# The MLP's second matrix as products of 400 and 264 columns, with the lesser operands of 128 tokens as weights

## The chip, the cores and the metric

The kernel runs on one core of one Trainium2 chip. The metric is the device time of one execution in microseconds (us), the median of several runs. A core has a tensor engine (PE, with its weight loads shown as PEld), a vector engine (DVE), a scalar engine (ACT), GpSimd (POOL) and SyncE (SP), which here only issues DMAs. Each engine works through its own instructions in order and waits for others by semaphores.

## The reference, cut to what matters

One step of a decoder with four layers, 264 tokens (256 of a prompt, 8 samples) and 1024 channels, all in float32. Each layer is a mixer (layers 0 and 3: gated short conv, 1: pooling, 2: Conformer conv), then an MLP:

```
x = x + mixer(rms_norm(x))
h = relu(rms_norm(x) @ mlp_w1)        # 1024 -> 4096
x = x + (h * h) @ mlp_w2              # 4096 -> 1024
```

At the end stands one more norm. The change concerns `(h * h) @ mlp_w2` in all four layers.

## The kernel before, in words

Channels lie on the 128 partitions and the 264 tokens along the free axis, so x is eight blocks of 128 x 264. TensorE takes float32 in its one-pass form only with a loss, so each number is split into a leading part (h, rounded) and a lesser part (l = number - h), and a product is three matmuls into one sum: whi with uh, whi with ul, wlo with uh (lines 160, 161, 162, the helper `mm`). The product of the two lesser parts is left out.

Weights come as a stream of units of 1024 rows x 256 columns (1 MB), in the order of their use: SP's DMA into `wst` (3 buffers), ACT's cast to `whi` (line 119), DVE's difference to `wlo` (line 120; POOL's in one mixer), into 5 buffers. Each unit is split in four pieces; `behind` issues some pieces (`pump`) behind each block of matmuls, and `done_units` allows the next unit's pieces. All of the order is written out by hand: what `behind` issues is in program order on each engine's queue.

The MLP goes in two halves of the hidden layer (h = 0, 1). In a half the first matrix makes 16 hidden blocks u (DVE line 1076, ACT 1082, split by ACT 225 and DVE 227). Then comes the stage of the second matrix (lines 1107 to 1120): for each of 4 pairs of output blocks (j), over 16 hidden blocks in two units (g), the 3 matmuls of 264 columns each for both blocks. When an output block is complete, `summed` adds it to x on DVE (line 1104 in the first half, `add_x`, line 532, in the second). In the second half `ready` follows: ACT scales x to xh (230) and squares it (242), DVE makes xl (232), POOL adds the squares in `acc` (243). The next mixer starts with `opening_unit`, which uses xh and xl block by block, and then a matmul on `acc` (272). There are 8 such stages. Behind the last stage `last_ready` (1218) squares and scales x, and `to_rows` (1204), queued in `later`, turns it with three transposes on PE (1212).

Layer 2's mixer runs a conv of 31 taps. DVE sums the taps of some blocks (855); PE takes those of the others by diagonal matrices (928 to 930), which ACT (814) and POOL (808) make one tap at a time (`make_diag`). They lie in places of other tiles (`diag_place`), and a new one is issued as a step uses one up.

## Time and profile before

| what | value |
|---|---|
| device time, median of 3 runs | 1126.05 us (1123.84 to 1126.81) |
| span of the profiled execution, first to last instruction | 1120.6 us |
| PE busy | 1101.6 us, 98%, 8981 matmuls |
| DVE, ACT, POOL busy | 762.3, 635.9, 197.7 us |
| chain that ended last | PE 91%, DVE 5%, ACT 2%, POOL 1% |
| DMA queue of the weights | 185.86 MB, 52.3% of 16 engines |

The span leaves out what lies before the first and behind the last instruction; the median of the runs is 5.45 us longer. The profiled execution has no time of its own beside its span. A matmul's busy time in a row (about 284 ns) is its way through the array; matmuls overlap, so the time that one takes from the next is read from the distance between starts, or from the length of a stretch over the number of matmuls in it.

### The profile page before, as it was taken

The page shows a single profiled execution, that of the slowest core. Times are in us where ns is not written, and L with a number is a line of the kernel's source. Part 1 is how long each engine was busy: PE and PEld are TensorE (multiplying, and loading weights), DVE is VectorE, ACT ScalarE, POOL GpSimd, SP SyncE. Part 2 cuts the span into 40 slices and gives each one's busy share as a digit, 9 for nine tenths or more (in the row PEclk, how much of TensorE's full clock was granted, in tenths as well). Part 3 has the DMA queues.
Part 4 walks back from the last instruction along what each step waited for, and adds up shares of the span by engine and source line. Part 5 has one row for each costly group of instructions (what it writes and reads, how often), then busy time and mean ns, then how long its engine had stood idle before and what let it go on. Part 6 is the DMA issues. An engine that isn't in the chain of part 4 may idle for free.

```text
span 1120.6 us, 22403 instructions
## 1 busy us (share of the span) xinstructions
PE 1101.6 (98%) x8981; PEld 1094.9 (98%) x8981; DVE 762.3 (68%) x1471; ACT 635.9 (57%) x1380; POOL 197.7 (18%) x363
## 2 busy tenths in 40 slices
PE   9999999999999999999999999999999999999997
PEld 8999999999999999999999999999999999999997
DVE  6878865566569647666998697467568687656731
ACT  5556663565458536644895686356545466535642
POOL 4212420100220000014895100000011120000010
PEclk9999999999999999999999999999999999999998
DMA  7666765555508666554440076655536555565511
GB/s 252 226 218 185 242 205 165 181 181 174 166 5 262 215 193 208 166 182 146 151 120 1 3 244 214 191 178 189 188 114 226 188 174 176 181 191 185 184 44 39
DMA packets 182792, 189.13 MB, mean 169 GB/s; under 512 B 3439, under 2 KB 181015, under 8 KB 182664
## 3 DMA queue, kind: packets, MB, share of 16 engines
q1 hardware_dynamic: 182288, 185.86, 52.3%
q0 software_dynamic: 384, 1.81, 0.5%
q8 instruction: 70, 1.15, 0.4%
q14 instruction: 34, 0.28, 0.1%
q10 hardware_dynamic: 16, 0.03, 0.0%
HBM read 186.27 MB, written 2.89 MB: 169 GB/s over the span
## 4 chain that ended last, share of the span: by engine, by line
PE 91%; DVE 5%; ACT 2%; POOL 1%; issue 0%; DMA 0%; SPq 0%; DVEq 0%; ACTq 0%
PE mm L160 28%; PE mm L162 28%; PE mm L161 28%; DVE mm L855 2%; PE mm L343 1%; ACT diag L814 1%; PE mm L341 1%; PE mm L344 1%; POOL wlo L120 1%; DVE gb L879 0%; PE mm L928 0%; POOL diag L808 0%; PE mm L929 0%; PE mm L930 0%; DMA vrows<-in_norm_mix_g_dram 0%
## 5 line engine op out<-in xcount | busy, mean ns | idle before, releaser
L119 ACT CAST whi<-wst 128x512 fp32r<-128x512 f32 x692 | 386.9, 616 | 250.1 <-PE mm L161 236.3
L120 DVE TENSOR_TENSOR wlo<-wst,whi 128x512 fp32r<-128x512 f32 x652 | 430.7, 705 | 99.6 <-ACT whi L119 91.7
L160 PE MATMUL mm<-xh,whi 128*128 128x264 f32 x1512 | 434.8, 288 | 3.1 <-DVE t L870 3.1
L162 PE MATMUL mm<-xh,wlo 128*128 128x264 f32 x1512 | 430.6, 285 | 0.0
L161 PE MATMUL mm<-xl,whi 128*128 128x264 f32 x1512 | 429.1, 284 | 0.0
L160 PE MATMUL mm<-uh,whi 128*128 128x264 f32 x1168 | 332.5, 285 | 0.0
L162 PE MATMUL mm<-uh,wlo 128*128 128x264 f32 x1168 | 331.6, 284 | 0.0
L161 PE MATMUL mm<-ul,whi 128*128 128x264 f32 x1168 | 331.1, 283 | 0.0
L160 PEld LDWEIGHTS mm<-xh,whi 128*128 128x128 f32 x1512 | 285.6, 189 | 4.1 <-DVE t L870 3.8
L161 PEld LDWEIGHTS mm<-xl,whi 128*128 128x128 f32 x1512 | 286.2, 189 | 0.2
L162 PEld LDWEIGHTS mm<-xh,wlo 128*128 128x128 f32 x1512 | 285.3, 189 | 0.0
L160 PEld LDWEIGHTS mm<-uh,whi 128*128 128x128 f32 x1168 | 220.0, 188 | 0.2 <-DVE xall L534 0.2
L161 PEld LDWEIGHTS mm<-ul,whi 128*128 128x128 f32 x1168 | 219.8, 188 | 0.0
L162 PEld LDWEIGHTS mm<-uh,wlo 128*128 128x128 f32 x1168 | 219.5, 188 | 0.0
L243 POOL TENSOR_TENSOR acc<-acc,sq 128x264 f32<-128x264 f32 x62 | 53.3, 860 | 552.2 <-ACT sq L242 551.4
L1076 DVE SCALAR_TENSOR_TENSOR t<-mm,r 128x264 f32<-128x264 f32 x128 | 55.1, 430 | 65.9 <-PE mm L162 65.8
L225 ACT CAST uh<-u 128x264 fp32r<-128x264 f32 x144 | 59.6, 414 | 32.1 <-DVE u L589 28.0
L1082 ACT ACTIVATE u<-t 128x264 f32<-128x264 f32 x128 | 54.1, 423 | 35.6 <-DVE t L1076 35.6
L855 DVE SCALAR_TENSOR_TENSOR mm<-gb,pv,mm 128x256 f32<-128x256 f32 x144 | 58.6, 478 | 7.1 <-POOL gb L878 2.5
L227 DVE TENSOR_TENSOR ul<-u,uh 128x264 fp32r<-128x264 f32 x144 | 61.6, 428 | 0.3
L532 DVE TENSOR_TENSOR xall<-mm,xall 128x264 f32<-128x264 f32 x48 | 20.6, 430 | 59.8 <-PE mm L162 59.8
L120 POOL TENSOR_TENSOR wlo<-wst,whi 128x512 fp32r<-128x512 f32 x40 | 53.2, 1356 | 21.0 <-ACT whi L119 21.0
(210 smaller groups left out, 826.0 us busy)
## 6 DMA issues: line engine op xcount, KB each, us to landing
wst<-in_mlp_w_dram SPq DMA_DIRECT2D x128, 1024.0 KB, 5.6
wst<-in_a_w_in_dram SPq DMA_DIRECT2D x23, 1024.0 KB, 5.4
wst<-in_c_w_pw_dram SPq DMA_DIRECT2D x12, 1024.0 KB, 5.5
wst<-in_a_w_out_dram SPq DMA_DIRECT2D x8, 1024.0 KB, 5.1
xin<-in_x_prompt_dram SPq DMA_DIRECT2D x2, 512.0 KB, 6.8
wst<-in_b_w_group_dram SPq DMA_DIRECT2D x1, 1024.0 KB
out_y_prompt_dram<-ys SPq DMA_DIRECT2D x4, 256.0 KB
stc<-in_state_conv_c_dram SPq DMA_DIRECT2D x2, 480.0 KB, 6.7
```

Source lines behind the costliest of these rows:

```text
L119: nc.scalar.copy(hi[:, k:k + 2], st[:, k:k + 2])
L120: (nc.gpsimd if u == 3 or (u, k) in ((0, 2), (0, 6)) else lo_engine[0]).tensor_tensor(out=lo[:, k:k + 2], in0=st[:, k:k + 2], in1=hi[:, k: ...
L160: nc.tensor.matmul(ps[:, :n], hi[:, k, s], xh[:, :n], start=first, stop=False)
L161: nc.tensor.matmul(ps[:, :n], hi[:, k, s], xl[:, :n], start=False, stop=False)
L162: nc.tensor.matmul(ps[:, :n], lo[:, k, s], xh[:, :n], start=False, stop=last)
L225: nc.scalar.copy(h, src)
L227: lambda: nc.vector.tensor_tensor(out=l, in0=src, in1=h.bitcast(F32), op=ALU.subtract)
L243: nc.gpsimd.tensor_tensor(out=acc, in0=acc, in1=sq, op=ALU.add)
L532: nc.vector.tensor_tensor(out=x[k], in0=ps[:, :T], in1=x[k], op=ALU.add)
L855: nc.vector.scalar_tensor_tensor(out=z(e), in0=gb[e][:, t:t + SEQ], scalar=col("ccw", t * 8 + e), in1=z(e), op0=ALU.mult, op1=ALU.add,)
L1076: nc.vector.scalar_tensor_tensor(out=t1, in0=ps[:, :T], scalar=0.0, in1=r, op0=ALU.max, op1=ALU.mult)
L1082: nc.scalar.activation(u, t1, AF.Square)
```

## The change

The hidden block's leading and lesser parts now lie side by side in one tile of 528 columns. Units of the second matrix have 512 rows and 512 columns. A stage has two quarters (q) of four output blocks each. Per hidden block and output block there are two matmuls: whi with 400 columns (264 leading ones and the lesser ones of the first 136 tokens), wlo with 264. The lesser parts of the last 128 tokens are the *weights* of one further matmul per hidden block, with the 512 columns of whi moving; its sums, tokens by outputs, lie in a bank `turned`. ACT copies these to `back` (two casts of 128 x 256), and one matmul with an identity for each output block (`turn`) adds them, turned back, to the block's last 128 columns. `summed` then adds two parts to x.

```diff
+OWN = T - 128
     def hidden(n):
-        return (
-            [act.tile([P, T], F32R, tag=f"uh{m}", name=f"uh{m}") for m in range(n)],
-            [act.tile([P, T], F32R, tag=f"ul{m}", name=f"ul{m}") for m in range(n)],
-        )
+        both = [act.tile([P, 2 * T], F32R, tag=f"u{m}", name=f"u{m}") for m in range(n)]
+        return [t[:, :T] for t in both], [t[:, T:] for t in both], both
...
             def summed(e, ps):
+                nc.vector.tensor_tensor(out=x[e][:, :OWN], in0=ps[:, T:T + OWN], in1=x[e][:, :OWN], op=ALU.add)
                 if h == 1:
                     return add_x(e, ps, ready)
...
-            for j in range(4):
-                ps2 = [psum(), psum()]
-                for g in range(2):
-                    w = next_unit()
-                    for c in range(2):
-                        for k in range(NB):
-                            kk = g * NB + k
-                            mm(ps2[c], w, c, k, uh[kk], ul[kk], T, kk == 0, kk == 15)
-                        if c == 1:
-                            done_units()
-                        if g == 0:
-                            behind(lambda c, ps: lambda: None, c, None)
-                        else:
-                            behind(summed, 2 * j + c, ps2[c], h == 1 and j == 3 and c == 1)
+            for q in range(2):
+                last_parts(h, q, both, summed)
+
+    def last_parts(h, q, both, summed):
+        turned, pss, back = psum(), [], []
+        def turn(c):
+            nc.tensor.matmul(
+                pss[c][:, OWN:T], back[c // 2][:, c % 2 * P:(c % 2 + 1) * P], ident_r, start=False, stop=True
+            )
+        for g in range(4):
+            hi, lo = (wide(t) for t in next_unit())
+            for k in range(4):
+                nc.tensor.matmul(
+                    turned, both[4 * g + k][:, T + OWN:], hi[:, k], start=g + k == 0, stop=g + k == 6
+                )
+            if g == 3:
+                for n in range(2):
+                    back.append(tmp.tile([P, 2 * P], F32R, tag="u", name="back"))
+                    nc.scalar.copy(back[n], turned[:, n * 2 * P:(n + 1) * 2 * P])
+            for c in range(4):
+                if g == 0:
+                    pss.append(psum())
+                s = slice(c * P, (c + 1) * P)
+                for k in range(4):
+                    t = both[4 * g + k]
+                    nc.tensor.matmul(pss[c][:, :T + OWN], hi[:, k, s], t[:, :T + OWN], start=g + k == 0, stop=False)
+                    nc.tensor.matmul(pss[c][:, :T], lo[:, k, s], t[:, :T], start=False, stop=False)
+                if c == 3:
+                    done_units()
+                ready_now = ()
+                if g == 3 and c > 0:
+                    for n in ((0, 1), (2,), (3,))[c - 1]:
+                        turn(n)
+                    ready_now = ((0, 1), (2,), (3,))[c - 1]
+                if not ready_now:
+                    behind(lambda c, ps: lambda: None, c, None, False, 1)
+                for n in ready_now:
+                    behind(summed, 4 * q + n, pss[n], h == 1 and q == 1 and n == 3, 1)
```

An ACT copy at the start makes the identity in the one-pass type (`ident_r`). Because the hidden tiles are now joined, the places of other tiles in them move too: the pooling mixer's rows, and in layer 2 the conv's diagonals, of which fewer are made before the conv, with a longer lead in it:

```diff
-                    for _ in range(4 if e < 4 else 3):
+                    for _ in range(3 if e < 7 else 2):
                         make_diag()
...
-            if made[0] - 16 <= taps.index((e, t)):
+            if made[0] - 20 <= taps.index((e, t)):
                 make_diag()
```

The order of PE in the last stage; before, in the first unit of the last pair, between the products for output block 6 and those for block 7 (`xall` is x, `ident` the identity, line 1212 the transposes of block 5):

```order
L160 MATMUL mm<-uh_13125,whi 128x264
L161 MATMUL mm<-ul_13141,whi 128x264
L162 MATMUL mm<-uh_13125,wlo 128x264
L1212 MATMUL mm<-ident,xall 128x128 x3
L160 MATMUL mm<-uh_13118,whi 128x264
L161 MATMUL mm<-ul_13134,whi 128x264
```

And now, in the last unit behind the second of its four output blocks (lines 1161 and 1162 are the two products, 1141 is `turn`, 1265 the transposes of x):

```order
L1161 MATMUL mm<-u_12472,whi 128x400
L1162 MATMUL mm<-u_12472,wlo 128x264
L1141 MATMUL mm<-ident_r,back 128x128 x2
L1265 MATMUL mm<-ident,xall 128x128 x3
L1161 MATMUL mm<-u_12469,whi 128x400
L1162 MATMUL mm<-u_12469,wlo 128x264
```

Before, block 5 was complete 24 matmuls ahead of its transposes; now the transposes are of block 4, whose last sums come from the first of the two matmuls of line 1141 right ahead of them.

The order of DVE at the end of layer 0's MLP, from output block 5's add on; before (532 is the add to x, 120 the weights' lesser parts, 232 makes xl):

```order
L532 TENSOR_TENSOR xall<-mm,xall 128x264
L120 TENSOR_TENSOR wlo<-wst,whi 128x512 x2
L232 SCALAR_TENSOR_TENSOR xl_133<-xall,pv,xh_125 128x264
L120 TENSOR_TENSOR wlo<-wst,whi 128x512 x2
L232 SCALAR_TENSOR_TENSOR xl_134<-xall,pv,xh_126 128x264
L120 TENSOR_TENSOR wlo<-wst,whi 128x512 x2
L532 TENSOR_TENSOR xall<-mm,xall 128x264
L120 TENSOR_TENSOR wlo<-wst,whi 128x512 x2
L532 TENSOR_TENSOR xall<-mm,xall 128x264
L232 SCALAR_TENSOR_TENSOR xl_135<-xall,pv,xh_127 128x264
L232 SCALAR_TENSOR_TENSOR xl_136<-xall,pv,xh_128 128x264
```

And now (1125 and 547 are the two adds to x, 128 the weights' lesser parts, 247 makes xl):

```order
L1125 TENSOR_TENSOR xall<-mm,xall 128x136
L547 TENSOR_TENSOR xall<-mm,xall 128x264
L128 TENSOR_TENSOR wlo<-wst,whi 128x512
L247 SCALAR_TENSOR_TENSOR xl_133<-xall,pv,xh_125 128x264
L1125 TENSOR_TENSOR xall<-mm,xall 128x136
L547 TENSOR_TENSOR xall<-mm,xall 128x264
L247 SCALAR_TENSOR_TENSOR xl_134<-xall,pv,xh_126 128x264
L1125 TENSOR_TENSOR xall<-mm,xall 128x136
L547 TENSOR_TENSOR xall<-mm,xall 128x264
L247 SCALAR_TENSOR_TENSOR xl_135<-xall,pv,xh_127 128x264
L247 SCALAR_TENSOR_TENSOR xl_136<-xall,pv,xh_128 128x264
```

The adds of blocks 4 to 7 moved together, each is two instructions, and the pieces of weights that lay between them moved ahead.

## Rows read from the trace of the kernel before

**Rows 1.** The page's busy times, and from its 40 slices PE's busy tenths and the clock granted to TensorE.

```profile
PE 1101.6 (98%) x8981; PEld 1094.9 (98%) x8981; DVE 762.3 (68%) x1471; ACT 635.9 (57%) x1380; POOL 197.7 (18%) x363
...
PE   9999999999999999999999999999999999999997
...
PEclk9999999999999999999999999999999999999998
```

**Rows 2.** Waits of PE alone, longest in total first (engine, line, tile, what it waited for: us in total, times, longest).

```profile
PE mm L160 <- DVE t L870: 3.1, 3, 1.9
...
PE mm L928 <- POOL diag L808: 1.0, 1, 1.0
...
PE st L949 <- POOL diag L808: 0.8, 1, 0.8
```

**Rows 3.** Windows of three of the eight stages of the second matrix (stretch, its length, busy us and instructions of PE, PEld, DVE, ACT, POOL, then clock, DMA share, GB/s); a stage has 384 matmuls, three more straddle its ends.

```profile
159.29:205.91 46.62, 46.62 (x387) 46.62 (x386) 24.20 (x42) 18.20 (x34) 0.00 (x0) 1.00 0.59 181
366.11:412.73 46.62, 46.62 (x387) 46.62 (x386) 25.40 (x45) 18.96 (x36) 0.00 (x0) 1.00 0.62 194
687.53:734.15 46.62, 46.62 (x387) 46.62 (x386) 24.21 (x42) 18.20 (x34) 0.00 (x0) 1.00 0.59 181
```

**Rows 4.** PE's timeline in the pooling mixer (start, busy, line, tile, rows*columns of the weights, moving partitions x columns): the first and the last of 24 matmuls with 128 columns of weights, of 12 with 48, and of 12 more with 48.

```profile
300.83 0.28 PE L633 MATMUL mm<-whi,xh 128*128 128x256 f32 x1
...
303.55 0.28 PE L635 MATMUL mm<-whi,xl 128*128 128x256 f32 x1
303.67 0.28 PE L633 MATMUL mm<-whi,xh 128*48 128x256 f32 x1
...
304.92 0.28 PE L635 MATMUL mm<-whi,xl 128*48 128x256 f32 x1
...
308.78 0.28 PE L633 MATMUL mm<-whi,xh 128*48 128x256 f32 x1
...
310.06 0.28 PE L635 MATMUL mm<-whi,xl 128*48 128x256 f32 x1
```

**Rows 5.** The chain that ended last in order of time (start, us, what), one piece: two matmuls of 264 columns in plain float32.

```profile
118.32 0.44 PE st L272 x2
```

**Rows 6.** PE's timeline: matmuls of 128 and 112 columns in the one-pass type behind one of 264.

```profile
320.03 0.22 PE L695 MATMUL mm<-band,yh 128*128 128x128 f32 x1
320.08 0.28 PE L695 MATMUL mm<-band,yl 128*128 128x128 f32 x1
320.19 0.27 PE L695 MATMUL mm<-band,yh 128*128 128x112 f32 x1
```

**Rows 7.** Groups of instructions by line and shape (busy us, mean ns of one, idle before).

```profile
L120 DVE TENSOR_TENSOR wlo<-wst,whi 128x512 fp32r<-128x512 f32 x652 | 430.7, 705 | 99.6 <-ACT whi L119 91.7
...
L1104 DVE TENSOR_TENSOR xall<-mm,xall 128x264 f32<-128x264 f32 x32 | 13.9, 433 | 38.0 <-PE mm L162 38.0
...
L712 DVE TENSOR_TENSOR mm<-mm,count 128x15 f32<-128x15 f32 x2 | 0.4, 182 | 0.2
...
L119 ACT CAST whi<-wst 128x512 fp32r<-128x512 f32 x692 | 386.9, 616 | 250.1 <-PE mm L161 236.3 <-issue 5.6 <-PE mm L162 4.4
...
L943 ACT COPY d<-mm 128x256 f32<-128x256 f32 x2 | 0.6, 354 | 0.0
```

**Rows 8.** Timeline at the end of layer 1's MLP (the adds of blocks 6 and 7, the two xl), the sum of squares' last add, and PE's matmul on it; then the same add and matmul behind layer 0's MLP.

```profile
506.93 0.43 DVE L532 TENSOR_TENSOR xall<-mm,xall 128x264 f32<-128x264 f32 x1 [1.08 <-PE mm L162]
...
509.85 0.43 DVE L532 TENSOR_TENSOR xall<-mm,xall 128x264 f32<-128x264 f32 x1 [1.29 <-PE mm L162]
...
510.32 0.52 ACT L230 ACTIVATE xh<-xall,pv 128x264 fp32r<-128x264 f32 x1 [2.09 <-DVE xall L532]
510.74 0.41 ACT L242 ACTIVATE sq<-xall 128x264 f32<-128x264 f32 x1
510.87 0.49 DVE L232 SCALAR_TENSOR_TENSOR xl<-xall,pv,xh 128x264 fp32r<-128x264 f32 x1 [0.19 <-ACT xh L230]
...
511.29 0.76 POOL L243 TENSOR_TENSOR acc<-acc,sq 128x264 f32<-128x264 f32 x1 [2.12 <-ACT sq L242]
...
515.50 0.61 PE L272 MATMUL st<-acc,ones 128*128 128x264 f32 x2
...
302.47 0.76 POOL L243 TENSOR_TENSOR acc<-acc,sq 128x264 f32<-128x264 f32 x1 [2.13 <-ACT sq L242]
...
305.04 0.89 PE L644 MATMUL st<-ones,acc 128*128 128x1 f32 x8
```

**Rows 9.** Timeline behind the last matmul of the last MLP.

```profile
1110.53 0.43 DVE L532 TENSOR_TENSOR xall<-mm,xall 128x264 f32<-128x264 f32 x1 [2.49 <-PE mm L162]
...
1110.65 0.73 PE L1231 MATMUL st<-ones,acc 128*128 128x1 f32 x6
1111.05 0.42 ACT L1222 ACTIVATE sq<-xall 128x264 f32<-128x264 f32 x1 [1.95 <-DVE xall L532]
1111.51 0.52 ACT L1223 ACTIVATE xall<-xall,pv 128x264 f32<-128x264 f32 x1
...
1112.22 0.53 PE L1212 MATMUL mm<-ident,xall 128*128 128x128 f32 x3
```

**Rows 10.** The chain in order of time, one piece in layer 2's mixer: ACT making four diagonals. Then ACT's first cast of x, from the timeline of the start (behind the brackets the idle time ahead of it).

```profile
540.54 2.44 ACT diag L814 x8
...
6.11 1.00 ACT L359 ACTIVATE xh<-mm,pv 128x264 fp32r<-128x264 f32 x2 [3.80 <-PE mm L357]
```

More of the change, by code (lines that the diff above doesn't have):

```diff
@@ L48, in unit, with wide_unit, wide @@
         return w[r0:r0 + 1024, c0:c0 + 256].rearrange("(k p) c -> p k c", p=P)
+    def wide_unit(w, r0, c0):
+        return w[r0:r0 + 512, c0:c0 + 512].rearrange("(k p) c -> p k c", p=P)
+    def wide(t):
+        return t.rearrange("p (k b) c -> p k (b c)", b=2)
     units = []
@@ L73, in mlp_units @@
                 units.append(unit(i["mlp_w1"][layer], 0, h * 2048 + j * 256))
-            for j in range(4):
-                for g in range(2):
-                    units.append(unit(i["mlp_w2"][layer], h * 2048 + g * 1024, j * 256))
+            for q in range(2):
+                for g in range(4):
+                    units.append(wide_unit(i["mlp_w2"][layer], h * 2048 + g * 512, q * 512))
     for layer in range(4):
@@ L99, in load_to @@
             else:
-                nc.sync.dma_start(out=t, in_=units[u])
+                nc.sync.dma_start(out=t if units[u].shape[1] == 8 else wide(t), in_=units[u])
             staged[u] = t
@@ L216, in decoder_trunk, with operands @@
     x = [xall[:, k, :] for k in range(NB)]
-    xh = [act.tile([P, T + DB], F32R, name=f"xh{k}") for k in range(NB)]
-    xl = [act.tile([P, T + DB], F32R, name=f"xl{k}") for k in range(NB)]
+    xh, xl = [], []
+    def operands():
+        for name, tiles in (("xh", xh), ("xl", xl)):
+            tiles[:] = [act.tile([P, T + DB], F32R, tag=f"{name}{k}", name=f"{name}{k}") for k in range(NB)]
+    operands()
+    ident_r = const.tile([P, P], F32R, name="ident_r")
+    nc.scalar.copy(ident_r, ident)
     acc = act.tile([P, T], F32, name="acc")
@@ L652, in mixer_b @@
         for k in range(NB):
-            t = act.tile([P, P], F32, tag=f"u{'hl'[k % 2]}{12 + k // 2}", name=f"keep{k}")
+            if k % 2 == 0:
+                pair_ = act.tile([P, 2, P], F32, tag=f"u{12 + k // 2}", name=f"keep{k}")
+            t = pair_[:, k % 2, :]
             nc.gpsimd.tensor_tensor(out=t, in0=x[k][:, T - P:T], in1=g_mix(k).to_broadcast([P, P]), op=ALU.mult)
@@ L833, in mixer_c @@
         dt = {}
-        gb = [act.tile([P, 30 + T], F32, tag=f"ul{NB + e}", name=f"gb{e}") for e in range(NB)]
+        gb = [act.tile([P, 30 + T], F32, tag=f"u{NB + e}", name=f"gb{e}") for e in range(NB)]
         zs = const.tile([P, NB, DB], F32, name="zs")
@@ L1032, in mixer_c @@
             nc.gpsimd.tensor_tensor(out=dt[e], in0=dt[e], in1=mu, op=ALU.subtract)
-        uh, ul = hidden(NB)
+        uh, ul, _ = hidden(NB)
         st = {}
@@ L1071, in mlp @@
         for h in range(2):
-            uh, ul = hidden(2 * NB)
+            uh, ul, both = hidden(2 * NB)
             def evac(m, ps):
@@ new lines, in last_parts @@
+    def last_parts(h, q, both, summed):
[4 more added lines that the diff above has]
+            )
+        for g in range(4):
+            hi, lo = (wide(t) for t in next_unit())
[26 more added lines that the diff above has]
+                    behind(summed, 4 * q + n, pss[n], h == 1 and q == 1 and n == 3, 1)
```

30 lines of the change are left out of this document (18 added, 12 removed).

## The prediction, made blind

> **What bounds the kernel now.** I read the page's busy times first, then its chain, PE's waits, and then the stages of the second matrix one by one. PE is busy 98% of the span, at a granted clock of 2.4 GHz in nearly all slices [rows 1], and its waits listed by releaser are a few us, nearly all outside the MLPs [rows 2]. So the kernel is one long queue of matmuls, and a change counts by what it adds to or takes from that queue, and by new waits put into it. The second matrix has eight stages of 384 matmuls; each takes 46.62 us without a gap [rows 3], that is 46.62 / 384 = 121.4 ns for a matmul of 264 columns. At 2.4 GHz 264 columns are 110.0 ns, so 11.4 ns of each are something else. I call it the surplus. Eight stages are 373.0 us of the span.
>
> **The products.** Per hidden block and four output blocks, before: 12 x 264 = 3168 columns. Now: 4 x 400 + 4 x 264 + 512 = 3168. The columns are equal, so nothing is saved in columns; 9 matmuls stand where 12 stood, and the saving is whatever part of the surplus belongs to a matmul and not to a column. There are 8 x 2 x 16 = 256 such groups: 1024 matmuls of 400, 1024 of 264, 256 of 512 columns for 3072 of 264.
>
> No row has 400 or 512 columns in this type, so I bound their surplus. With 256 columns (106.7 ns) and 128 columns of weights, 23 distances make 303.55 - 300.83 = 2.72 us, 118.3 ns, surplus 11.6. With 48 columns of weights, 11 distances make 1.25 us once and 1.28 us once, 115.0 ns on average, surplus 8.3 [rows 4]. A weight load that ends far before the columns do thus lowers the surplus by some 3 ns, but does not remove it. The lowest row is two plain float32 matmuls, 0.44 us for 2 x 264 columns [rows 5]: if they take two clocks per column they have no more than some 2 ns each above their columns, but that is another mode. In a matmul of 400 columns the weights have 57 ns more than now to be ready; I take the middle of 8.3 and 11.4, 9.9 ns, and keep both ends.
>
> - 1024 x (166.7 + 9.9) = 180.8 us; 256 x (213.3 + 9.9) = 57.1 us; 1024 x 121.4 = 124.3 us. Together 362.2, against 373.0: **-10.8 us**.
> - With 8.3 it is -12.8, with 11.4 it is -8.8, with 2 it is -20.9. If the surplus goes with columns, it is 0.
>
> The Trainium skill (TensorE: Matmul & The Clock Gate, section Back-to-back issue gap) gives a matmul's distance as its columns over 2.4 GHz plus 2.5 ns. By that figure 264 columns would take 112.5 ns; the row shows 121.4, so the rule does not hold here as it stands, but if its 2.5 ns are all that belongs to a matmul, the rest goes with columns, and 768 matmuls fewer are an estimated 1.9 us. That speaks for the second rival below.
>
> **The turns back.** 64 matmuls of 128 columns, four a quarter: two in a row, then one and one. In the one-pass type the first of 128 columns behind one of 264 is followed after 0.05 us, the next after 0.11, when its follower waits for its weights [rows 6]. Per quarter 0.05 + 0.11 + 2 x 0.06, some 0.29 us; 16 quarters **+4.6 us**. If every turn cost 0.11 it would be 7.0.
>
> They wait for ACT's two copies to `back`. Ahead of these on ACT's queue are at most two casts of weights (0.62 each) that the end of the unit before frees; the copies are about 0.35 each [rows 7]. That is 1.9 us, against 4 x 0.22 of products with 512 columns and two blocks of 4 x (176.6 + 121.4) = 1.19 us, together 3.3. So the turns find their operand ready, with 1.3 us to spare. ACT is busy 18 to 19 of 46.6 us in these stages [rows 3]; behind the copies wait casts, which PE needs a unit or more later.
>
> **The ends of layers.** DVE gets one more add per output block. By 264 columns at 433 ns and 15 at 182 [rows 7], 136 columns are an estimated 300 ns, 64 of them 19 us on an engine that is idle almost half of each such stage: hidden, but for the last four blocks of a layer. Their sums used to come 2.9 us apart; now blocks 4 and 5 come at once, 6 and 7 1.2 us apart. Count from the first pair. ACT and DVE need for each block two adds (0.73), scale 0.52, square 0.41, xl 0.49 [rows 8], and two pieces of weights lie between (0.62 and 0.70). Hand over hand down both queues, block 7's xl is done at about 6.8 us and the squares' sum on POOL (0.76) at 7.4. The next mixer begins at 2.5, wants xl of block 7 after 42 matmuls, at 7.6, and the sum at 8.3: both in time, with 0.8 us to spare. Without that cover each us late would be a us at two layer ends. In the pooling mixer PE asks for the sum after 4.2 us [rows 8], at 6.7, so PE waits 0.7 there; I put **+0.5 us**, from 0 to 1.5.
>
> **The end of the kernel.** Here the order shows PE's transposes of block 4 right behind the turns that complete it, and PE stands still until x is added, squared and scaled. Behind the last matmul that way takes DVE's add at 1110.53 to the transpose at 1112.22, some 2.0 us with the matmul's own end, and 0.25 more for the second add: PE stands for about 2.1. Behind the turn of block 6 it stands 0.6 more, of which 0.2 remain, and the last block's two adds cost 0.25 [rows 9]. Together **+2.5 us**; from 1.5 to 3.2.
>
> **Layer 2's mixer.** Four diagonals fewer are ready as the conv begins, and ACT makes them inside it. Four take 2.44 us [rows 10], and PE waits for diagonals already now, 1.0 us once [rows 2]. On the other side the lead in the conv grows from 16 to 20 steps, POOL's first diagonal stands behind one piece of weights fewer, and ACT has less to do in the part before, where PE waited 3.1 us for DVE [rows 2]. I take **+0.5**, from -1.5 to +2.4. The extra table load and copy at the start lie in ACT's 3.8 idle us ahead of its first cast [rows 10]: nothing. DMAs of 2 KB rows instead of 1 KB carry the same bytes at 59% of the engines' time in a stage [rows 3]: nothing.
>
> **The sum.** -10.8 + 4.6 + 0.5 + 2.5 + 0.5 = -2.7 us; the profiled span of 1120.6 becomes 1117.9. With the 5.45 us by which the median is longer than the span: 1123.3 us. A change within 0.3% (3.4 us) is about what cannot be told from none.
>
> **The rivals.**
>
> - *The surplus vanishes under long products.* If a weight load that ends early and a long stream leave only some 2 ns, the products save 20.9: 1126.05 - 20.9 + 8.1 = 1113.3 us. For it speaks the float32 pair [rows 5], against it that 48 columns of weights still leave 8.3 [rows 4]. Chance 0.17.
> - *Slower: the surplus goes with columns.* TensorE would then take some 0.46 ns per column of this type, at any length. 256 and 264 columns (118.3 and 121.4) fit this as well as a fixed 11.5 ns. The products save nothing, and the turns, the tail and the two mixers stay: 1126.05 + 8.1 = 1134.1 us. It decides from where a matmul of 400 columns takes over 181 ns: there the saving falls below what is added less 3.4 us. Against it: two lengths of weights at one length of columns differ by 3 ns, so at least that is not the columns'. Chance 0.20.
> - *The turns wait for ACT.* If another two casts stand ahead of the copies, PE waits perhaps 0.5 us in 16 quarters, 8 us on top of the forecast: 1131 us. ACT's whi casts wait 236 us for PE in all [rows 7], so a queue behind PE is its normal state; against it stands the spare 1.3 us. Chance 0.08.
>
> The forecast has 0.55; its own range is 1119.5 to 1127.5.
>
> **Range and chances.** From the second rival's short of its end to the first's: 1112 to 1133. Faster by over 0.3%: all of the first rival (0.17) and 0.25 of the forecast (where the surplus is nearer 8.3, or layer 2 gains); within: 0.28 of the forecast, 0.03 of the second and 0.02 of the third; slower: 0.02, 0.17 and 0.06. So 0.42, 0.33, 0.25.
>
> **What would show it.** The distance from a matmul of 400 columns to the next: 175 to 178 ns right, 169 the first rival, 183 the second. The stage's length: 45.9 us ((362.2 + 4.6) / 8) against 46.62; 44.6 or 47.2 for the rivals. PE's waits list should have no `back`, one wait of about 2 us for ACT line 1276 near the end, and one of under a us in the pooling mixer. Wrong would be waits at all quarters, or a conv of layer 2 that is longer by more than 2.5 us.

## The result: slower, and the profile after

The changed kernel took 1136.24 us (median of four runs, 1133.70 to 1138.68) against 1124.94 for the kernel before on the same chip (1122.24 to 1126.81): a ratio of 1.0106, 95% interval 1.0083 to 1.0128, so 9 to 14 us slower. Forecast were 1123.3 and a range of 1112 to 1133. The profiled execution of the changed kernel has a span of 1132.0 us, 11.4 more than before's 1120.6; the difference of the medians is 11.3, so I look for it in the two traces. In every run that is on record with its own span the time is about 1.7 us above it; of the 5.45 us that the prediction added to the span, the other 3.7 say only that the traced execution of the kernel before was quicker than the median. That changes no difference.

The page's busy times and clock; they answer to [rows 1].

```profile
PE 1106.4 (98%) x8277; PEld 1087.9 (96%) x8277; DVE 774.4 (68%) x1534; ACT 647.4 (57%) x1414; POOL 198.4 (18%) x364
...
PEclk9999999999999999999999999999999999999998
```

704 matmuls fewer, and yet PE is busy 4.8 us more; the other 6.6 us of the span are idle. The same three stages as in [rows 3], by windows (length, then busy us and instructions of PE, PEld, DVE, ACT, POOL, clock, DMA share, GB/s):

```profile
157.44:204.68 47.24, 47.24 (x298) 45.84 (x297) 25.23 (x48) 19.49 (x38) 0.00 (x0) 1.00 0.58 179
366.05:413.31 47.26, 47.26 (x299) 45.85 (x297) 26.54 (x52) 20.37 (x41) 0.00 (x0) 1.00 0.62 194
691.12:738.36 47.24, 47.24 (x298) 45.84 (x297) 25.23 (x48) 19.50 (x38) 0.00 (x0) 1.00 0.57 179
```

Each stage is 0.62 us longer than before (46.62), without a gap in PE. PE's waits, in place of [rows 2]:

```profile
PE mm L1265 <- ACT xall L1276: 4.2, 4, 1.8
PE mm L168 <- DVE t L892: 2.9, 2, 1.9
PE st L971 <- POOL diag L830: 2.8, 1, 2.8
...
PE st L658 <- POOL rv L655: 0.3, 1, 0.3
```

Two are new in size: the transposes of x in the last stage (L1265) wait four times, twice for 1.8 us; and the first mean behind layer 2's conv (L971, before L949) waits 2.8 us where it waited 0.8. No turn waits for ACT's copies: `back` isn't in the list.

By the starts of the phases in the two traces, the 11.4 us are made up so:

| stretch | before | after | difference |
|---|---|---|---|
| start, to the first product of layer 0's output matrix | 88.85 | 86.90 | -1.95 |
| eight stages of the second matrix, without what stands at the end of the last | 8 x 46.62 | 8 x 47.24 | +5.0 |
| rest of the last stage, to the last matmul | 4.12 | 8.74 | +4.6 |
| layer 2's mixer | 107.02 | 109.58 | +2.6 |
| pooling mixer | 65.28 | 65.78 | +0.5 |
| everything else | | | +0.7 |

The start is not the change's. In the eight profiles of kernels with the changed kernel's start, that phase begins anywhere from 86.8 to 92.4 us. What differs is the granted clock: the trace of the kernel before has a stretch at 1.2 GHz there, the changed kernel's has none. The same 3.41 us in both, before first (18 matmuls against 31):

```profile
35.12:38.53 3.41, 3.41 (x18) 3.41 (x17) 2.44 (x6) 3.37 (x8) 0.91 (x2) 0.50 0.59 205
35.12:38.53 3.41, 3.41 (x31) 3.41 (x30) 2.48 (x6) 3.37 (x8) 0.92 (x2) 1.00 0.45 153
```

Of the eight profiles, the two without such a stretch between 35 and 42 us reach the phase at 86.8 and 86.9, the six with one at 88.9 to 92.4. So the -1.95 us is the luck of one traced execution.

### The profile page after: what moved, and what is told of

It is laid out like the page before. It is cut to its first block, busy times and chain, and to the rows that moved or that the text cites. A ratio compares the mean times of both kernels' runs of the same rounds, so it can differ in the third digit from the quotient of the medians.

```text
span 1132.0 us, 21175 instructions
## 1 busy us (share of the span) xinstructions
PE 1106.4 (98%) x8277; PEld 1087.9 (96%) x8277; DVE 774.4 (68%) x1534; ACT 647.4 (57%) x1414; POOL 198.4 (18%) x364
## 4 chain that ended last, share of the span: by engine, by line
PE 90%; DVE 5%; ACT 2%; issue 1%; DMA 1%; POOL 1%; SPq 0%; ACTq 0%; DVEq 0%; POOLq 0%
PE mm L168 17%; PE mm L1161 16%; PE mm L170 16%; PE mm L169 16%; PE mm L1162 11%; PE mm L1148 5%; DVE mm L877 2%; PE mm L358 1%; PE mm L359 1%; PE mm L356 1%; PE mm L950 1%; PE mm L952 1%; PE mm L951 1%; DMA xin<-in_x_prompt_dram 1%; ACT whi L127 1%
## 5 line engine op out<-in xcount | busy, mean ns | idle before, releaser
L128 DVE TENSOR_TENSOR wlo<-wst,whi 128x512 fp32r<-128x512 f32 x651 | 426.4, 697 | 158.5 <-ACT whi L127 153.0
L1161 PE MATMUL mm<-u,whi 128*128 128x400 f32 x1024 | 317.7, 347 | 0.0
L1162 PE MATMUL mm<-u,wlo 128*128 128x264 f32 x1024 | 291.0, 284 | 0.0
L1162 PEld LDWEIGHTS mm<-u,wlo 128*128 128x128 f32 x1024 | 192.9, 188 | 2.9
L1161 PEld LDWEIGHTS mm<-u,whi 128*128 128x128 f32 x1024 | 192.5, 188 | 2.8
L240 ACT CAST u<-u 128x264 fp32r<-128x264 f32 x144 | 59.5, 413 | 32.6 <-DVE u L603 28.5
L1148 PE MATMUL mm<-whi,u 128*128 128x512 f32 x256 | 70.1, 395 | 0.0
L242 DVE TENSOR_TENSOR u<-u,u 128x264 fp32r<-128x264 f32 x144 | 61.4, 427 | 0.3
L245 ACT ACTIVATE xh<-xall,pv 128x264 fp32r<-128x264 f32 x56 | 28.9, 516 | 41.3 <-DVE xall L547 25.7
L1148 PEld LDWEIGHTS mm<-whi,u 128*128 128x128 f32 x256 | 43.8, 188 | 5.6
```

What stands on the lines that cost most here:

```text
L128: (nc.gpsimd if u == 3 or (u, k) in ((0, 2), (0, 6)) else lo_engine[0]).tensor_tensor(out=lo[:, k:k + 2], in0=st[:, k:k + 2], in1=hi[:, k: ...
L240: nc.scalar.copy(h, src)
L242: lambda: nc.vector.tensor_tensor(out=l, in0=src, in1=h.bitcast(F32), op=ALU.subtract)
L1148: nc.tensor.matmul(turned, both[4 * g + k][:, T + OWN:], hi[:, k], start=g + k == 0, stop=g + k == 6)
L1161: nc.tensor.matmul(pss[c][:, :T + OWN], hi[:, k, s], t[:, :T + OWN], start=g + k == 0, stop=False)
L1162: nc.tensor.matmul(pss[c][:, :T], lo[:, k, s], t[:, :T], start=False, stop=False)
```

## The experiments

**How long one matmul takes from the next, alone.** A kernel of nothing but series of matmuls of one shape, for instance:

```diff
+    for n in (256, 264, 320, 400, 512):
+        series(x, st, n, 128)
+    series(x, st, 400, 128, alt=264)
```

> Only series of 48 matmuls of one shape each, on rounded weights, with nothing else running; none of the reference is computed. One-pass float32 with 128 columns of weights and 256, 264, 320, 400, 512 moving columns; 256 and 512 with 48 columns of weights; 512 with 64 of 128 partitions; bfloat16 with 256 and 512; 400 and 264 in turns. Theory A (the time of a one-pass float32 matmul goes with its columns, 0.45 to 0.46 ns each, with some 3 ns for the matmul): 264: 121 ns, 320: 146, 400: 183, 512: 233, and the same when 400 and 264 alternate (304 a pair). Theory B (the changed kernel's surroundings made its long matmuls slow; alone they have a fixed surplus of about 10 ns): 320: 143, 400: 177, 512: 223. If the reading of four-byte numbers is what costs, bfloat16 has 109 and 216 ns and half the partitions change nothing or little.

Windows of four series of 48 each: 264, 400 and 512 columns, then 512 columns in bfloat16.

```profile
24.66:30.43 5.77, 5.77 (x51) 5.77 (x49) 0.00 (x0) 0.00 (x0) 0.00 (x0) 1.00 0.00 0
...
37.47:46.12 8.65, 8.65 (x51) 8.65 (x49) 0.00 (x0) 0.00 (x0) 0.00 (x0) 1.00 0.01 2
46.12:57.01 10.89, 10.89 (x49) 8.95 (x49) 0.00 (x0) 0.00 (x0) 0.00 (x0) 1.00 0.00 0
...
90.59:100.92 10.33, 10.32 (x48) 4.88 (x48) 0.00 (x0) 0.00 (x0) 0.00 (x0) 1.00 0.00 0
```

Within the series a matmul starts 120.0 ns after the last with 256 or 264 columns, 146.7 with 320, 180.0 with 400, 226.7 with 512. These are whole numbers of 6.67 ns, the time of 16 columns at 2.4 GHz: 18, 18, 22, 27 and 34 steps, which is the columns divided by 16, rounded down, plus two. So there is a surplus that doesn't grow with columns, but it is 13.3 ns at 256, 320, 400 and 512 columns and 10.0 at 264, where the half step of 8 columns comes free. The matmul that the change removes is the one with the smallest surplus, and those that it puts in its place have a larger one. So neither theory fits as put: A fails at 512 (233) and at 256 and 264, which cost the same, and B has the fixed part 3 ns too small. In bfloat16 256 and 512 columns took 109.0 and 216.0 ns. The Trainium skill (TensorE: Matmul & The Clock Gate, section Back-to-back issue gap) gives, for the gap of a single matmul, its columns over 2.4 GHz plus 2.5 ns, that is 109.2 and 215.8; the bfloat16 series agree, the one-pass float32 ones don't. With 48 columns of weights 256 columns took 117 ns, 3 less than with 128, but 512 took 234 to 235, 8 more; from half the partitions 512 took 227 as the median. 400 and 264 columns in turns took 191.5 + 121.6 here, against 300.0 for the two alone.

**Three products again.** The changed kernel with the old three products in its new order (the products with 512 columns, the copies and the turns are gone):

```diff
-                    nc.tensor.matmul(pss[c][:, :T + OWN], hi[:, k, s], t[:, :T + OWN], start=g + k == 0, stop=False)
-                    nc.tensor.matmul(pss[c][:, :T], lo[:, k, s], t[:, :T], start=False, stop=False)
+                    nc.tensor.matmul(pss[c][:, :T], hi[:, k, s], t[:, :T], start=g + k == 0, stop=False)
+                    nc.tensor.matmul(pss[c][:, :T], hi[:, k, s], t[:, T:], start=False, stop=False)
+                    nc.tensor.matmul(pss[c][:, :T], lo[:, k, s], t[:, :T], start=False, stop=g + k == 6)
```

> The changed kernel with its wide units, joined tiles and quarters, but the products as before: three of 264 columns per hidden block and output block, no weights made of lesser operands, no turns, one add. It computes all of the reference. Theory A (time goes with columns, so the new products save nothing and the turns are what is added): a stage falls from 47.24 us to 46.6, the whole to 5 to 7 us below the changed kernel, and stays 3 to 5 us above the kernel before for layer 2's mixer and the end. Theory B (the products save 1.3 us a stage and another part of the change, units or tiles, costs 1.9): a stage rises to 48 us or more, and the whole is slower than the changed kernel.

1130.97 us, ratio to before 1.0063 (1.0041 to 1.0085). A stage takes 46.8 to 46.9 us, the last stage 51.92, layer 2's mixer 110.5. By the medians the new order, units, tile places and the longer lead together cost over half of the loss, without any new product; the same 384 matmuls take 0.2 us a stage more than in the old order. The whole is 5.3 us below the changed kernel, as theory A has it, but 7.4 above the kernel before, where A has 3 to 5; theory B's 48 us a stage didn't come. In the trace only 1.5 us more lie in the first seven stages together; the two mixers are 3.5 and 1.4 us longer than before, with 6.8 and 3.4 us at 1.2 GHz in them.

**No turns.**

```diff
-                    for n in ((0, 1), (2,), (3,))[c - 1]:
-                        turn(n)
```

> The changed kernel without the 64 matmuls that turn the sums back; so the lesser operands of the last 128 tokens are left out of the output, and copies and adds stay. Theory A: a stage falls by 8 turns, 0.6 us, to 46.65, the whole by 4.7 us or a little more at the end. Rival (the turns cost their wait for ACT's copies as well): a stage falls by more than 1 us. Rival (the stage's extra time is in the long products): it falls by less than 0.3 us.

1129.8 us, ratio 1.005 (1.0031 to 1.007). One stage in its window, where the changed kernel has 47.24:

```profile
159.82:206.22 46.40, 46.40 (x291) 45.01 (x290) 25.35 (x49) 19.50 (x38) 0.00 (x0) 1.00 0.59 182
```

Eight turns are worth 0.84 us, 0.105 each, 6.7 in all: more than the 0.6 of theory A, and under the 1 us from which waits for the copies would have to be thought of. What is left, the new products in their order, is 0.22 us a stage below before: 1.8 us in all. Held against the three products in the same new order (46.8 to 46.9), the new products save 0.42 us a stage on average, 3.4 in all, which is what the steps of the first sweep give; half of that is lost again to the new order, units and places, if it isn't one of the shifts without a known cause that are told below.

**The lead in layer 2's conv back at 16.**

```diff
-            if made[0] - 20 <= taps.index((e, t)):
+            if made[0] - 16 <= taps.index((e, t)):
```

> The changed kernel with the lead of diagonals in layer 2's conv back at 16 steps; 28 diagonals before the conv as changed. Theory: ACT's two copies for the first mean stand behind four more diagonals with a lead of 20, and PE waits 2.8 us for them; with 16 that wait is 1.0 to 1.5 us and the mixer 1.5 to 2.5 us shorter, the whole 1.5 to 3 us faster. Rival (the four diagonals that were not made ahead are the loss): the wait stays, or another of the same length comes earlier in the conv, and the whole is within 1 us of the changed kernel.

1134.31 us, ratio 1.0089 (1.0072 to 1.0107). The mixer in its windows, first the changed kernel,

```profile
510.69:620.27 109.58, 101.67 (x796) 99.41 (x796) 93.48 (x203) 78.18 (x213) 80.90 (x114) 0.98 0.31 98
```

then with the lead of 16:

```profile
516.25:623.16 106.91, 100.60 (x796) 98.14 (x795) 93.49 (x203) 77.99 (x213) 80.87 (x114) 1.00 0.32 101
```

2.7 us less, and as long as before (107.02). The times of the two runs differ by 1.9 us, within what they scatter; the stretch is what shows it. The trace says how the lead costs. The timeline of the changed kernel where the mean waits, ACT's rows and PE's:

```profile
588.92 1.28 ACT L836 ACTIVATE diag<-ident,wd 128x128 fp32r<-128x128 f32 x4
...
590.08 0.64 ACT L965 COPY d<-mm 128x256 f32<-128x256 f32 x2
...
590.60 0.91 PE L971 MATMUL st<-d,ones 128*128 128x264 f32 x3 [2.77 <-POOL diag L830]
```

PE's last conv matmul ahead of it began at 587.54. The wait is put down to a diagonal of POOL, but the mean needs `d`, and what ends last ahead of it is the first of ACT's two copies. ACT copies the finished sums (L965) only behind the diagonals that the longer lead put ahead of the copies; with a lead of 16 PE stands 1.73 us there instead of 3.06. Behind the longer wait of the changed kernel lie 3.4 us at a granted clock of 1.2 GHz (591.8 to 595.2), which the run with 16 doesn't have: that is the other 1.1 us of PE's busy time. One version below (the transposes held back, lead of 20) has the same wait, 3.05 us, but no such stretch in its trace, and parts the two:

```profile
514.28:622.34 108.06, 100.28 (x797) 97.96 (x796) 93.44 (x203) 78.19 (x213) 80.78 (x114) 1.00 0.32 100
```

So of the 2.7 us the lead itself is 1.2 and the clock behind it 1.5. Four of the five traces with a lead of 20 have the low clock there, none of the three with 16. The four diagonals fewer cost nothing.

**Pairs of lengths, alone and beside other engines.** Another kernel of series, 96 matmuls each, the last six beside casts, differences and loads:

```diff
+    for ns in ((400, 264), four, (400, 256), (384, 264), (384, 256), (512, 264), (264, 264, 264, 128)):
+        series(x, st, ns, 128)
```

> Only series of 96 matmuls each in the one-pass float32 type, with 128 columns of weights where nothing else is said; all else is left out. The first nine series run with the other engines idle: 400 and 264 columns in turns; four of 400, then four of 264; 400 and 256; 384 and 264; 384 and 256; 512 and 264; three of 264 and one of 128; 400 and 264 with 48 columns of weights; 400 and 264 from two sources. Then 264, 264, 400, 512, 400 and 264 in turns, and fours, beside casts on ACT, differences on DVE and a stream of loads. In the first sweep a lone length took 120.0 (264) and 180.0 ns (400), in turns 191.5 and 121.6. Theory H (half a step: distances go in steps of 16 columns, and 264 is 16.5 of them, so that what follows a 264 is off by half a step): 400 beside 256 and 384 beside 256 cost what they cost alone (300 and 293 for the pair), fours cost 1200 to 1215 for eight, 48 columns of weights change nothing (313). Theory W (a longer matmul behind a shorter one waits for its weights): every pair of unlike lengths costs some 10 ns more than its parts, 400 and 256 about 311, fours about 1210 for eight, and with 48 columns of weights 300. Theory B (surroundings): the quiet series are as cheap as alone or as in the first sweep, and the same series beside the other engines cost 1 to 3% more: 264 at 121.5, 400 at 184, 512 at 232.

Windows: 400 and 264 in turns with the rest idle; the same from two sources; 400 alone beside ACT, DVE and loads; 400 and 264 beside them.

```profile
19.94:34.34 14.40, 14.40 (x97) 14.40 (x96) 0.00 (x0) 0.00 (x0) 0.00 (x0) 1.00 0.00 1
133.90:148.62 14.72, 14.72 (x98) 14.72 (x97) 8.58 (x14) 9.17 (x15) 0.00 (x0) 1.00 0.36 103
171.67:188.95 17.28, 17.28 (x98) 17.28 (x97) 16.46 (x25) 16.46 (x27) 0.00 (x0) 1.00 0.63 199
210.76:225.16 14.40, 14.40 (x97) 14.40 (x96) 13.72 (x21) 13.71 (x23) 0.00 (x0) 1.00 0.57 172
```

48 pairs in 14.40 us are 300.0 ns a pair, exactly the two alone, with the others idle or at 57% of the DMA engines. That refutes both the weights' wait (400 and 256: 300; 48 columns of weights change little) and surroundings of this kind as the cause of the kernel's 306.5 for a pair, and the half step of theory H too, by which turns would stay at 313. It also shows that a pair has no one price: the first sweep had 313 for the same lengths, and two sources in turns cost 306.7 (that series ran partly beside the others). One matmul of 128 columns among three of 264 costs 111 ns: the fours take 471.4 where three are 360. In the kernel a turn is worth 0.105 us, nearly the same.

**The order within a block.** Four matmuls of 400, then four of 264, instead of in turns:

```diff
                     nc.tensor.matmul(pss[c][:, :T + OWN], hi[:, k, s], t[:, :T + OWN], start=g + k == 0, stop=False)
+                for k in range(4):
+                    t = both[4 * g + k]
                     nc.tensor.matmul(pss[c][:, :T], lo[:, k, s], t[:, :T], start=False, stop=False)
```

> The changed kernel with the products of a block in another order: of a unit's four hidden blocks first the four matmuls of 400 columns, then the four of 264. Nothing is left out. If the surplus of 400 columns comes from following a 264, three of four fall from 184.9 to about 180, 0.6 us a stage with a little less for the first: stage 46.7, device time 1136.2 - 4 = 1132. If it comes from the surroundings (casts, loads), 400 stays at 184 to 185, the stage at 47.2 and the time at 1136.

1141.03 us, ratio 1.016 (1.0135 to 1.0184): 5 us slower than the changed kernel, which neither theory expected. The stage is 47.20 us, the same within 0.04, so following a 264 isn't what makes a 400 dear. The windows of a stage and of the two places in the last stage behind the waits for ACT:

```profile
162.55:209.75 47.20, 47.20 (x298) 45.78 (x297) 25.24 (x48) 19.86 (x39) 0.00 (x0) 1.00 0.59 178
1095.50:1102.40 6.90, 5.09 (x27) 4.94 (x26) 3.40 (x8) 3.23 (x7) 1.69 (x2) 0.75 0.01 4
1124.00:1129.70 5.70, 3.89 (x19) 3.73 (x18) 1.85 (x6) 1.77 (x4) 1.50 (x2) 0.70 0.00 0
```

After standing for 2.09 us PE was granted 1.2 GHz for 3.4 us, both times; that is the 2.6 us by which the last stage is longer (58.59 against 55.98). The changed kernel's traced execution stands as long at the same places, and its clock stays at 2.4 GHz; why the one falls and the other not is open. Another 2.0 us lie in code that wasn't touched: the first matrix behind four of the stages, 47.18 and 47.17 us for 46.56 in the last two layers. The edit moves no tile, so places in memory alone don't explain that. The traced execution is the longest of the four (1143.27 us) and its start is 5.1 us longer than the changed kernel's, so the clock's part in the 5 us between the medians isn't measured.

**Transposes held back, and both mends.** The transposes in the last stage wait until two more blocks are done:

```diff
+                lag[0] = 2 if ready_now else 0
                 for n in ready_now:
                     behind(summed, 4 * q + n, pss[n], h == 1 and q == 1 and n == 3, 1)
+                lag[0] = 0
+                if g == 3 and c == 3 and q == 0:
+                    run_later(1)
```

> The changed kernel with the transposes of x in the last stage held back by two blocks, so that none stands right behind the turn that completes its block. Nothing is left out. If the two stalls behind the turns (2.1 us each, and 0.5 each for block 6) are what the end costs, the last stage goes from 55.98 to about 51.6 us and the time to 1132. If PE only waits elsewhere (the transposes pile up behind the last products, four blocks of three), it gains under 1.5 us: 1135.

> The same, and the lead in layer 2's conv back at 16. Nothing is left out. If the two add up: 1136.2 - 4.4 - 2.6 = 1129.2, still slower than before by about 0.4 to 0.5%, which is what the turns (6.7) less what the products save (1.8) come to. If the mixers' share was chance, it stays at 1132.

Late alone: 1133.87 us, ratio 1.0094 (1.0066 to 1.0123); the last stage is 54.38 us instead of 55.98, a gain of 1.6, by which the rival (waits that move elsewhere) is nearly right. With the lead of 16: 1129.3, ratio 1.0055 (1.0035 to 1.0076). That is the number that was expected (1129.2), but by luck: the sum had 4.4 for the last stage, and its trace shows 2.0. PE's waits in that version:

```profile
PE st L971 <- POOL diag L830: 1.4, 1, 1.4
...
PE st L1288 <- POOL acc L258: 0.9, 1, 0.9
...
PE mm L1161 <- ACT ys L1271: 0.5, 1, 0.5
```

The 4.2 us for L1276 are gone, and 1.4 of them come back as two waits: for the rows' copy that frees a bank (L1271) and, at the very end, for the sum of squares (L1288). The last 1.4 us before the last matmul also run at 1.2 GHz, and 2.2 us in the version with a lead of 20; the changed kernel's clock falls only behind its last matmul. The last stage is 54.00 us, 2.0 less.

**Both mends and no turns.**

> The version with late transposes and a lead of 16, without the turns: the lesser parts of the last 128 tokens are multiplied but not added to x, all else is computed. If turns (6.7 us) are what keeps that version above the kernel before, its 1129.3 becomes 1122.6, no different from 1122.8 to 1123.6. If the turns' cost was in the stalls behind them, which that version has mostly lost already, it gains 4 or less: 1125 to 1127.

1125.42 us (ten runs), ratio 1.0024 (1.001 to 1.0038). Against the version with turns (1.0055) that is 0.31%, 3.5 us, less than the 6.7 expected, which lies just outside what the two intervals together allow (0.7 to 6.3). It lies where the rival had it, but not for the rival's reason: the stages do fall to 46.40, the last to 52.13, together 7.75 us. The two traces are ill matched. The one without turns is of the longest of ten executions (1129.08 us; the four with a mean granted clock of 0.992 took 1127.0 to 1129.1, the other six 1123.8 to 1125.5), the one with turns of the shortest of four. So they show where time can come back, and not how the medians come about. The first matrix in layer 2's second half (384 matmuls of 264 columns), with turns:

```profile
735.47:782.03 46.56, 46.56 (x386) 46.56 (x386) 32.40 (x66) 29.37 (x62) 0.00 (x0) 1.00 0.57 182
```

and without, in its second line the pooling mixer:

```profile
738.92:786.04 47.12, 47.12 (x386) 47.12 (x385) 32.13 (x64) 29.37 (x62) 0.00 (x0) 1.00 0.55 180
304.52:371.66 67.14, 67.14 (x535) 66.16 (x534) 53.64 (x123) 44.38 (x102) 13.38 (x24) 0.97 0.41 133
```

The same 384 matmuls take 122.7 ns each instead of 121.3, because of nothing in their own code; four such stretches give back 1.8 us, the same in all three kernels without turns (47.1 us each here). The pooling mixer has 3.4 us at 1.2 GHz and is 1.35 longer than with turns. From the first output product to the last matmul, 4.7 us are left; the start, longer by 5.6 us in this execution, more than takes them.

**The product loops alone.** What sets the kernel's 306.5 a pair, if not other engines? The two loops on fixed data, all else idle:

```diff
+    two_pairs()
+    quarter()
+    two_pairs()
+    quarter()
+    quarter(one=True)
+    quarter(wides=False)
+    quarter(n=392)
```

> Only the product loops of the two kernels, on fixed data, with all other engines idle; all else is left out. In order: the products of four output blocks as before has them, 192 matmuls of 264 columns, and one quarter of the changed kernel without its turns, 144 matmuls, then both again; the quarter with one hidden block as the source of all; the quarter without the 512 columns; the quarter with 392 for 400; then series of 264 columns: one source, two sources, weights from two tiles, 16 sources, 16 sources from their second half; 400 columns from 16 sources; 512 columns with weights from 16 tiles. Theory S (distances go in steps of 16 columns at 2.4 GHz, 6.67 ns: 18 for 264, 27 for 400, 34 for 512, and the kernels' excess of 1 to 3% over them comes with changing tiles, as the pair from two sources in the sweep of pairs, 306.7 for 300.0): the loops alone take what they take in the kernels, 192 x 121.4 = 23.3 us and 23.2 us (46.40 / 2); 392 columns save one step of 64 matmuls, 0.43 us; the series from one source stay at 120.0 and those from 16 are above. Rival (the excess is made by what else runs in the kernel): 23.04 us, and 64 x 180.0 + 64 x 120.0 + 16 x 226.7 = 22.83 us, and all series at 120.0, 180.0 and 226.7.

Windows of the first, second, fifth and seventh:

```profile
23.92:47.12 23.20, 23.20 (x194) 23.20 (x192) 0.00 (x0) 0.00 (x0) 0.00 (x0) 1.00 0.01 1
47.12:70.21 23.09, 23.09 (x146) 22.42 (x145) 0.00 (x0) 0.00 (x0) 0.00 (x0) 1.00 0.00 1
116.51:139.41 22.90, 22.90 (x147) 22.22 (x145) 0.00 (x0) 0.00 (x0) 0.00 (x0) 1.00 0.00 1
158.83:181.66 22.83, 22.83 (x147) 22.16 (x146) 0.00 (x0) 0.75 (x2) 0.00 (x0) 1.00 0.02 6
```

23.20 and 23.09: the new products save 0.11 us a quarter, 16 x 0.11 = 1.8 us, the same number as from the kernel without turns. Both loops are 0.11 us a quarter longer inside the kernels (23.31 and 23.20), so something in the kernels, the work beside them or the places of the tiles, costs both alike; which isn't shown. The measured loops lie between theory S (23.3 and 23.2) and the rival (23.04 and 22.83). On 392 theory S is wrong, 0.27 saved for 0.43, and on the sources too: 264 columns from one source took 121.3 ns, from two 120.1. By steps they would be 23.04 and 22.83; the excess over that is larger in the new loop (0.26 against 0.16), and 0.19 of it goes when all comes from one source. 400 columns from 16 sources took 183.3 ns, 512 columns with weights from 16 tiles 231.7, against 180.0 and 226.7 in the first sweep; 264 from 16 sources 120.8.

**Orders and places.** The loop of before in five orders and from sources at other places, all else idle:

```diff
+    loop(three(0, 2, 1))
+    loop(three(1, 0, 2))
+    loop(each(0, 1, 2))
+    loop(both_blocks)
+    loop(hi_then_lo)
+    loop(base, at(0, 272))
+    loop(base, at(8, 280))
+    loop(base, at(0, 264))
+    loop(base, at(16, 304))
```

> Only the product loop of the kernel before (192 matmuls of 264 columns for four output blocks), on fixed data, with all other engines idle, in other orders and from sources at other places; all else is left out. In order: as it is, twice; whi with uh, wlo with uh, whi with ul; whi with ul first; all eight blocks of whi with uh, then all with ul, then wlo; the two output blocks in turns; whi with uh and ul for all eight, then wlo; then the order as it is from wider tiles that hold both parts, starting at columns 0 and 272, 8 and 280, 0 and 264, 16 and 304. By steps of 16 columns it would be 192 x 120.0 = 23.04 us; as it is it took 23.20. Theory P (where a source starts within 16 columns decides: tiles of 264 columns start half a step off every second time): 0 and 272, 8 and 280 and 16 and 304 give 23.04, 0 and 264 gives 23.2 or more, the orders change nothing. Rival (what follows what decides): orders differ by 0.1 us or more, one of them 23.05 or less, and the places give 23.2. If one saves over 0.1 us, the kernel before would gain 0.1 / 192 = 0.5 ns for each of its some 7700 matmuls of this kind, 4 us.

Windows of the loop as it is, the two output blocks in turns, and the places 0 and 272, 0 and 264, 16 and 304 (the last has 191 distances):

```profile
24.53:47.73 23.20, 23.20 (x194) 23.20 (x192) 0.00 (x0) 0.00 (x0) 0.00 (x0) 1.00 0.01 1
...
140.53:164.06 23.53, 23.53 (x195) 23.53 (x193) 0.00 (x0) 0.00 (x0) 0.00 (x0) 1.00 0.00 1
187.47:210.76 23.29, 23.29 (x195) 23.29 (x193) 0.00 (x0) 0.00 (x0) 0.00 (x0) 1.00 0.00 1
234.08:257.15 23.07, 23.07 (x194) 23.07 (x193) 0.00 (x0) 0.00 (x0) 0.00 (x0) 1.00 0.00 1
257.15:280.07 22.92, 22.92 (x193) 22.92 (x192) 0.00 (x0) 1.12 (x3) 0.00 (x0) 1.00 0.06 19
```

Three orders take 23.20 like the present one, two take more. Orders matter by up to 0.33 us, and places too, from 120.0 ns a matmul (16 and 304) to 121.5 (8 and 280), but not by where a source starts within 16 columns: 0 and 272 is among the worst, 0 and 264 among the best. Both theories as put have fallen; the rule is open. In the whole kernel, 0 and 264 are the places of the joined tiles (528 columns wide there, 576 here): with them the three products took 46.8 to 46.9 us a stage, no less than 46.62. The best one, 16 and 304, wasn't tried there. No run found a version faster than the kernel before.

## Why the prediction was wrong, point by point

**The products: the step that failed.** It put -10.8 us, from one surplus of 9.9 ns for every new matmul, between bounds of 8.3 and 11.4. Measured are -1.8, by the kernel without turns and by the loops alone. The mechanism (a surplus that belongs to a matmul and not to its columns) held in the uniform series, but its size was wrong at both ends. Alone, a new matmul of 400 or 512 columns has 13.3 ns and the removed one of 264 has 10.0, so by steps a group of twelve matmuls becomes 4 x 180.0 + 4 x 120.0 + 226.7 = 1426.7 for 1440 ns: 3.4 us in all, not 10.8. From 16 sources, the long ones go further over their steps (183.3 and 231.7) than the short ones (120.8), and in the kernel without turns 400 and 512 columns take 183.5 and 232 ns, where 176.6 and 223.2 were put. Why they do is open. That the new order and tiles could themselves lengthen a stage was put at nothing, without a reason; by the kernel with three products it was 0.2 us a stage, some 1.7 in all. The upper bound of 11.4 was taken from the very matmul whose surplus is smallest, and the thought that a longer matmul gives its weights more time pointed the wrong way.

Of the rivals for the products, a surplus of 2 ns was far off. The other, a surplus that goes with columns, had a price (0) near what came; its time, 1134.1, was the nearest number given, and its stage of 47.2 us is the one measured. In the changed kernel 400 columns take 184.9 ns and 264 take 121.6, above the 181 from which it was to decide. That is in part luck: its mechanism is not what the series show (256 and 264 columns cost the same), and its stage comes out right because the turns cost 2.1 us more than it had and the products save 1.8. A pair from the timeline of a stage: seven pairs in 201.84 - 199.70 = 2.14 us, 306 ns.

```profile
199.70 0.35 PE L1161 MATMUL mm<-u,whi 128*128 128x400 f32 x1
...
201.84 0.34 PE L1141 MATMUL mm<-ident_r,back 128*128 128x128 f32 x2
```

The lower bounds also fell: the 8.3 of a row with 48 columns of weights doesn't carry to long matmuls, since at 512 columns such weights took 8 ns more and not 3 less. The 2 ns rested on a misread row: [rows 5] is one sum of squares, issued as two instructions (14 for the program's seven sums).

**The turns: under-counted.** +4.6 was put, with 7.0 if every turn cost 0.11; it is 6.7. Taking the first at 0.05, as in [rows 6], counted only its own distance; a turn's price is what it adds to the stage, with what its follower waits. The upper end was the right one for all of them.

**The turns' operand: right.** The copies were in time in all quarters.

**The ends of layers: right.** +0.5 in the pooling mixer was forecast and 0.5 came; PE stands there from 304.42 to 304.98, at L658, behind POOL's last add to the sum of squares. At the other ends PE waits for nothing new.

**The end of the kernel: half seen.** +2.5 was put, +4.6 came. The mechanism was the one described, PE standing 2.1 us behind the turn that completes block 4. But a stage has two quarters, and the same order of code stands at the end of the first, behind block 0; the prediction read one place of two.

```profile
1088.61 0.34 PE L1141 MATMUL mm<-ident_r,back 128*128 128x128 f32 x2
1090.75 0.55 PE L1265 MATMUL mm<-ident,xall 128*128 128x128 f32 x3 [1.81 <-ACT xall L1276]
```

**Layer 2's mixer: past the end of its range.** +0.5 from -1.5 to +2.4 was put, +2.6 came, just over the 2.5 that the prediction itself named as a sign of being wrong. The longer lead was booked as a gain; it is the loss, 1.2 us through ACT's copies that stand behind the extra diagonals, and 1.5 through the low clock behind that wait. The diagonals that are no longer made ahead, booked as the loss, cost nothing with a lead of 16.

**The sum.** -1.8 for -10.8, +6.7 for +4.6, +0.5 as put, +4.6 for +2.5, +2.6 for +0.5: 12.6 instead of -2.7, less 1.95 us of a start whose clock didn't fall in that run, plus 0.7 of shifts elsewhere. Of the error of 14 us, the products are 9.0, and the three under-counted terms 6.3; the lucky start takes off 1.95.

## What to carry to other kernels

Before matmuls are merged, measure the distance of the lengths that come and of the one that goes: a surplus read at one length may be smallest exactly there, and here nine matmuls for twelve saved 7 ns in 1450. A short matmul in a stream of long ones added 105 to 111 ns here, twice the 53 ns of its columns at 2.4 GHz; the weight loads around such a matmul start some 110 ns apart (320.03, 320.14, 320.25 in the trace of before), so its price is likely that of the load, which no run here changes by itself. Compare traces of executions whose granted clocks are alike: one stretch of 3.4 us at 1.2 GHz made a phase 1.3 to 2 us longer here. Where a change re-orders what completes when, read the order at each place that repeats it, and ask what stands ahead of the releasing instruction on its own queue.

## What the runs showed of the hardware that was not expected

- One-pass float32 matmuls with 128 columns of weights, in the first sweep's uniform series, start a whole number of 6.67 ns apart: columns over 16, rounded down, plus two. 256 and 264 columns cost the same 120.0 ns. With 48 columns of weights (117 ns) or from 16 sources (120.8, 183.3, 231.7) they don't keep to such steps.
- The same lengths in turns took 300.0, 306.7 or 313 ns a pair in three series, and the same 384 matmuls 46.29 us before and 47.12 in a kernel that changed another stage. Places of the sources move it by 1.3%, the order of the products by 1.4%; what decides was not found.
- Casts, differences and 63% of the DMA engines' time beside a series of 400 columns didn't slow it at all (180.0 ns).
- A wait of 2.1 us was followed by 3.4 us at 1.2 GHz in one traced execution and by none in another, at the same place; a wait of 3.1 us (layer 2's first mean with a lead of 20) by such a stretch in four of five.
